# Moving a residual spill, half of a modulation part, two weight casts and one attention step inside the mixer of an encoder layer

## The chip, the core and the metric

The kernel runs on one core of one Trainium2 chip. The metric is the device time of one execution in microseconds (us); the median of three executions is 1164.8 us (1164.51 to 1168.15).

TensorE (PE in the profile, with its weight loads as PEld) multiplies, VectorE (DVE) and ScalarE (ACT) work on elements, GpSimd (POOL) helps with elements and issues some transfers, and SyncE (SP) issues most transfers. Each engine has a queue of its own that it works off strictly in order.

## The reference

One layer of an encoder for 512 prompt tokens and 32 sample tokens, all in float32, width 1024:

```python
mod = silu(c) @ w_cond + b_cond            # nine parts of 1024: shift, scale, gate of three blocks
x = LN(ALPHA*x + 0.5*(1+g1) * swiglu1(modulate(x, sh1, sc1)))
h = modulate(x, sh2, sc2)
rq,rk,rv,rg, aq,ak,av, iq,ik,iw = split(h @ w_in)
o_ret = head_norm(retention(rope(rq), rope(rk), rv)) * silu(rg)
s     = sum_h iw[h] * relu(iq[h] @ ik.T)   # indexer: scores of keys, 8 heads
o_att = attention over the top-k keys by s only
x = LN(ALPHA*x + (1+g2) * concat(o_ret, o_att) @ w_out)
x = LN(ALPHA*x + 0.5*(1+g3) * swiglu2(modulate(x, sh3, sc3)))
```

The gate g3 is part 8 of the modulation, the last of the nine. It is first needed after the second feed-forward block's products with gate and up weights.

## The kernel before

**Layout and precision.** Activations lie transposed, 128 channels on the partitions and the 544 tokens along the free side, in two halves of 272 tokens. Each float32 operand is split exactly into two parts, hi and lo, and a product is three matmuls (`mm3`, hi·hi, hi·lo, lo·hi). A weight tile of 128 columns and 1024 rows is therefore 24 matmuls for each half: 8 steps along the inner side, three matmuls each. All matmuls carry line 77 and all transposes line 80, because helpers issue them.

**Weights.** `fetch_w` loads a raw tile of 512 KB into one of three `wr` buffers from SP's queue. `split_w` makes the two parts in one of five `wh` buffers: ACT casts the raw tile to hi (L131), ACT writes minus hi into lo (L137), and POOL issues a transfer that adds the raw tile from memory into lo (L138). So lo is there only once this transfer has landed. `next_w` keeps three split tiles ahead of the one in use: the project that begins now also issues load, cast and transfer of the tile that is used three projects later.

**Order of the work.** The order on PE is written out by hand: `mm` and `turned` chain every PE instruction behind the one before. `load` chains the loads of SP's queue in the same way, in the order of the program. The other queues are ordered by the framework, which places an instruction by its place in the program and by its own reckoning of when the operands are there; `add_manual_dep(..., NOSYNC)` adds an order between two instructions and no wait. Side work runs as generators: `tick()` is called after each half of a project, and a generator that yields n is resumed n ticks later. What it then issues stands on PE's queue behind the half just done. In the mixer a tick is one half of a project, 24 matmuls.

**The mixer** (between the two feed-forward blocks) projects h with 33 tiles of `w_in`: first the indexer's key and queries, then for four retention heads query, key and value (`retention`), then for four attention pairs key, query and value (`pair_inputs`), then four gates. Alongside run:

- `cond_ahead(8)`, part 8 of the modulation. It loads eight row blocks `wc` of 512 KB and sums them, weighted, into two accumulators `ca` on DVE: two instructions of 128x1024 elements for each block (L587 and L589). The first four blocks are loaded from POOL's queue, the last four from SP's. `cond_done` then reduces the accumulators on DVE in four pieces (L546, L547) and with one matmul.
- `spill`: the residual `xr` (four tiles, 544 KB each) is written to memory and read back at the gates (`reload`).
- `queries` and `index_query`: the rotary part goes through small transfers (`rp`), DVE and back, then parts are made (L694 on ACT, L695 on DVE) and small copies run on POOL (L776).
- `indexer`: for each of ten steps (t, c) 12 or 6 matmuls for each pair of heads into two banks, one in tag `l` (two buffers) and one in tag `o` (one buffer). ACT takes each through relu (L814), and DVE sums them (L821, L823). The next step's second bank is free only after the relu of the second head of the pair (s = 1) has read it.
- `topk` on DVE (L853, L854), then `attention`: twelve steps (pair c, group n) of logits, softmax on DVE and ACT, transposes and values. A step of pair c may begin once `roped` has set the flag ("stack", c).

Tiles of all these kinds share one pool `up` of 35 buffers.

The tick count of the mixer, followed by hand through the code: `cond_ahead` is spawned at tick 130; the first four blocks are added at tick 132, the last four loaded at tick 140 and added at ticks 140, 144, 148 and 152; `cond_done` reduces at ticks 158 to 161. The spill is issued at tick 144, the indexer's step (1, 0) at tick 145 and (2, 0) at tick 146. `roped` of pair 0 runs at ticks 169 to 171, logits (0, 0) at tick 172.

Of the kernel before, what the change touches and what calls it, by code (L numbers as in the profile page):

```python
# [13 lines left out]
ALU = mybir.AluOpType  # L14
# [4 lines left out]
ND = D // P  # L19
# [20 lines left out]
def encoder_layer_kernel(ctx, tc, xT, cT, wc1, w_e, w_cond, b_condT, lnp, w_gu1, w_dn1, w_in, w_out, w_gu2, w_dn2,  # L40
                         ckT, cv, cikT, s0, cmat, ropes, dec, csm,
                         yT, akT, avT, ikT, st_p, st_s):
    nc = tc.nc
# [22 lines left out]
    last = {}  # L66
# [58 lines left out]
    def split_w(raw, n, name, lo_eng=None, pool=None, pin=False, src=None):  # L125
        if pool is None:
            hl = wh.tile([P, 2, ND, P], FR, name=f"wh_{name}", tag="wh")
            hi, lo = hl[:, 0], hl[:, 1]
        else:
            hi, lo = (pool.tile([P, ND, P], FR, name=f"wu_{name}", tag="u") for _ in range(2))  # L130
        c = nc.scalar.copy(hi[:, :n, :], raw[:, :n, :])  # L131
        if "relu" in last:
            tc.add_manual_dep(c.ins, last.pop("relu"), NOSYNC, reason="order of issue")
        if pin:
            tc.keep_in_program_order(c)
        if src is not None and lo_eng is None:
            nc.scalar.mul(lo[:, :n, :], hi[:, :n, :].bitcast(F32), -1.0)  # L137
            nc.gpsimd.dma_start(lo[:, :n, :], src, accum_op=ALU.add)  # L138
        else:
            r = (lo_eng or nc.gpsimd).tensor_tensor(lo[:, :n, :], raw[:, :n, :], hi[:, :n, :].bitcast(F32), op=ALU.subtract)  # L140
            last["lo"] = r.ins.name
        return hi, lo
# [7 lines left out]

    stream = []
    split = []
    fetched = []

    def fetch_ahead():
# [421 lines left out]
    def cond_ahead(m):  # L577
        acc = [up.tile([P, 1024], F32, name=f"ca{m}_{r}", tag="u") for r in range(2)]

        def part(d):  # L580
            return w_cond[d * P:(d + 1) * P, 1024 * m:1024 * m + 1024]

        def add(d, w):
            for r in range(2):
                c = cz[:, d, r:r + 1]
                if d == 0:
                    nc.vector.tensor_scalar(acc[r], w, c, None, op0=ALU.mult)  # L587
                else:
                    n = nc.vector.scalar_tensor_tensor(acc[r], w, c, acc[r], op0=ALU.mult, op1=ALU.add)  # L589
                    if d > 4:  # L590
                        tc.add_manual_dep(n.ins, last["pe"], NOSYNC, reason="pace")

        ws = [up.tile([P, 1024], F32, name=f"wc{m}_{d}", tag="u") for d in range(4)]
        for d in range(4):
            nc.gpsimd.dma_start(ws[d], part(d))
        yield 1
        for d in range(4):
            add(d, ws[d])
        yield 8
        for d in range(4, ND):  # L600
            ws.append(up.tile([P, 1024], F32, name=f"wc{m}_{d}", tag="u"))
            load(ws[d], part(d))
        for d in range(4, ND):
            add(d, ws[d])
            yield 4
        spawn(cond_done(m, acc))

    def known(*ms):
# [191 lines left out]
    def indexer():  # L800
        nc.vector.memset(work[0], 0.0)
        nc.vector.memset(work[0][0:64, 64:128], NEG)
        flags.add(("mask", 0))
        yield 0
        for t, c in ((1, 0), (2, 0), (1, 2), (2, 1), (2, 2), (2, 3), (3, 0), (3, 1), (3, 2), (3, 3)):
            L = P * (t + 1)
            acc = work[t]
            n = 512 // L
            pair = [bank("l", "isc"), bank("o", "isc")]
            pair_products([[p[:, L * e:L * e + L] for e in range(n)] for p in pair],  # L810
                          [(iq[c + e], iks, t) for e in range(n)])
            for s in range(2):
                rl = scr("rl")
                r = nc.scalar.activation(rl[:, :n * L], pair[s][:, :n * L], AF.Relu)  # L814
                if (t, c) == (1, 0):
                    last["relu"] = r.ins.name
                for e in range(n):
                    hh = 2 * (c + e) + s
                    r, f = rl[:, L * e:L * e + L], iw[:, t, hh:hh + 1]
                    if hh == 0:  # L820
                        nc.vector.tensor_scalar(acc, r, f, None, op0=ALU.mult)  # L821
                    else:
                        nc.vector.scalar_tensor_tensor(acc, r, f, acc, op0=ALU.mult, op1=ALU.add)  # L823
            yield 1
            if c + n == 4:
                nc.vector.memset(acc[0:64, L - 64:L], NEG)
                flags.add(("score", t))
                if t == 1:
                    spawn(topk())
        psA, psB = bank("a", "iss"), bank("o", "iss2")  # L830
        for g in range(2):
            ps, p2 = bank("l", "isg"), bank("t", "isg2")
            lq = iqz[:, 128 * g:128 * g + 128]
            mm(ps, lq, cik, start=True, stop=True)
            mm(p2[:, 0:32], lq, ikn, start=True, stop=True)
            rl = scr("rls")
            nc.vector.tensor_scalar(rl[:, 0:512], ps, 0.0, iws[:, g:g + 1], op0=ALU.max, op1=ALU.mult)
            nc.vector.tensor_scalar(rl[:, 512:544], p2[:, 0:32], 0.0, iws[:, g:g + 1], op0=ALU.max, op1=ALU.mult)
            yield 1
            mm(psA, sel, rl[:, 0:512], start=(g == 0), stop=(g == 1))  # L840
            mm(psB[:, 0:32], sel, rl[:, 512:544], start=(g == 0), stop=(g == 1))
        nc.scalar.copy(work['s'][:, 0:512], psA)
        nc.scalar.copy(work['s'][:, 512:544], psB[:, 0:32])
        flags.add(("score", 's'))
# [19 lines left out]
    project(taken(qs[3]))  # L864

    def spill():
        yield 3
        for j in range(4):
            load(xd[j], xr[j].rearrange("p a t -> p (a t)"))

# [156 lines left out]
    def pair_inputs(c):  # L1027
        qk = unit("aqk")
        k, q = qk[:, 0, :], qk[:, 1, :]
        st = [unit("aqs", FR), unit("aks", FR)]  # L1030
        V = unit("aV")
        kn = V[:, 1, 64:96]
        qz = V[:, 1, 0:64]
        nc.gpsimd.memset(qz, 0.0)

        rp = unit("rp")

        def roped():
            yield 0
            rope_turn(rp, k, q)  # L1040
            nc.sync.dma_start(akT[c], k)
            yield 1
            parts(st[1], k)
            nc.gpsimd.tensor_copy(kn, k[:, TP:T])
            parts(st[0], q)
            for s in range(2):
                nc.gpsimd.tensor_copy(qz[own(s), 32 * s:32 * s + 32], q[own(s), TP:T])
            yield 1
            flags.add(("stack", c))

        Vs[c] = V
        stacks[c] = st
        for slot, z in enumerate((k, q)):
            project(taken(z))
            rope_gather(rp, slot, z)
        spawn(roped())
        value_chunk(V[:, 0, 0:512], V[0:32, 1, 128:256], avT[c], ("pair", c))

# [553 lines left out]
```

## Time and profile before

| what | value |
|---|---|
| time, median of three executions | 1164.8 us |
| the profiled execution's own time | 1163.95 us |
| its span, first to last instruction | 1162.1 us |
| PE busy | 1131.8 us (97%) |
| DVE busy | 785.7 us (68%) |
| ACT busy | 620.5 us (53%) |
| POOL busy | 202.9 us (17%) |
| mean granted clock of PE | 0.99 |

Busy shares are taken over the span. A row of the timeline gives start, length, engine, line, operation and tiles (written tile, arrow, read tiles) of one group, how many instructions it merges, and in brackets how long the engine stood before it and what released it. A row of the waits gives the waiting engine, tile and line, the releaser, the sum, the number and the longest. A row of the windows gives the stretch, its length, and for each engine busy time and count, then the granted clock of PE (1.00 is full), the share of time in which the transfer engines were busy, and GB/s. Rows marked SPq are issues of transfers on SP's queue, not their landing.

### The profile page before, as it was taken

The page shows a single profiled execution, that of the slowest core. Times are in us where ns is not written, and L with a number is a line of the kernel's source. Part 1 is how long each engine was busy: PE and PEld are TensorE (multiplying, and loading weights), DVE is VectorE, ACT ScalarE, POOL GpSimd, SP SyncE. Part 2 cuts the span into 40 slices and gives each one's busy share as a digit, 9 for nine tenths or more (in the row PEclk, how much of TensorE's full clock was granted, in tenths as well). Part 3 has the DMA queues.
Part 4 walks back from the last instruction along what each step waited for, and adds up shares of the span by engine and source line. Part 5 has one row for each costly group of instructions (what it writes and reads, how often), then busy time and mean ns, then how long its engine had stood idle before and what let it go on. Part 6 is the DMA issues. An engine that isn't in the chain of part 4 may idle for free.

```text
span 1162.1 us, 22904 instructions
## 1 busy us (share of the span) xinstructions
PE 1131.8 (97%) x9203; PEld 1099.8 (95%) x9203; DVE 785.7 (68%) x1738; ACT 620.5 (53%) x1064; POOL 202.9 (17%) x229
## 2 busy tenths in 40 slices
PE   8999999999999999799999999999999999999995
PEld 7999999999999999688989988999999999999995
DVE  5667674772569387588988777689877777821416
ACT  3545444443435435465655758654776667753523
POOL 0122111111211301432311101110211111061110
PEclk9999999999999999899999999999999999999998
DMA  9899999986999746874664757871777777478842
GB/s 357 291 290 317 255 263 230 243 218 165 299 276 240 160 175 155 273 175 119 147 149 84 193 177 210 227 193 66 157 180 166 180 183 175 116 224 192 178 83 78
DMA packets 71739, 228.26 MB, mean 196 GB/s; under 512 B 8688, under 2 KB 12912, under 8 KB 71632
## 3 DMA queue, kind: packets, MB, share of 16 engines
q0 software_dynamic: 23184, 77.87, 37.8%
q1 hardware_dynamic: 48304, 148.79, 36.2%
q8 instruction: 72, 1.18, 0.4%
q14 instruction: 35, 0.29, 0.1%
q10 hardware_dynamic: 144, 0.14, 0.0%
HBM read 215.16 MB, written 9.58 MB: 193 GB/s over the span
## 4 chain that ended last, share of the span: by engine, by line
PE 88%; DMA 5%; DVE 4%; ACT 1%; POOL 1%; issue 1%; SPq 0%; DVEq 0%; POOLq 0%; ACTq 0%
PE dn L77 26%; PE gu L77 23%; PE in L77 14%; PE pA L77 9%; PE pB L77 5%; DMA we_raw<-in_w_e 3%; PE pC L77 2%; PE gu_e L77 2%; PE po L77 1%; PE pt L80 1%; PE lg L77 1%; DMA wh_w<-in_w_in 1%; DMA rp<-iqf 1%; PE ro L77 1%; PE isc L77 1%
## 5 line engine op out<-in xcount | busy, mean ns | idle before, releaser
L77 PE MATMUL dn<-hid,wh_w 128*128 128x272 f32 x2112 | 266.8, 288 | 0.0
L77 PE MATMUL gu<-h,wh_w 128*128 128x272 f32 x2112 | 265.8, 288 | 0.0
L77 PEld LDWEIGHTS dn<-hid,wh_w 128*128 128x128 f32 x2112 | 265.4, 188 | 0.2
L77 PEld LDWEIGHTS gu<-h,wh_w 128*128 128x128 f32 x2112 | 264.9, 188 | 0.0
L77 PE MATMUL in<-h,wh_w 128*128 128x272 f32 x1392 | 190.7, 294 | 4.4 <-DMA wh_w<-in_w_in 3.9
L77 PEld LDWEIGHTS in<-h,wh_w 128*128 128x128 f32 x1392 | 179.9, 191 | 10.3 <-DMA wh_w<-in_w_in 4.2
L131 ACT CAST wh_w<-wr_w 128x1024 fp32r<-128x1024 f32 (+1 forms) x126 | 128.0, 1019 | 113.3 <-PE dn L77 87.7
L572 DVE SCALAR_TENSOR_TENSOR ca<-wc,cz,ca 128x1024 f32<-128x1024 f32 x84 | 106.4, 1294 | 25.7 <-DMA wc<-in_w_cond 25.6
L137 ACT ACTIVATE wh_w<-wh_w 128x1024 fp32r<-128x1024 f32 (+1 forms) x116 | 119.6, 1033 | 2.2
L138 POOL DMA_DIRECT2D wh_w<-in_w_gu x43 | 37.8, 878 | 201.6 <-ACT wh_w L137 162.0
L138 POOL DMA_DIRECT2D wh_w<-in_w_dn x42 | 37.0, 893 | 183.9 <-ACT wh_w L137 175.6
L281 DVE SCALAR_TENSOR_TENSOR xs<-dn,C,xs 128x272 f32<-128x272 f32 (+2 forms) x24 | 9.0, 404 | 81.2 <-PE dn L77 81.2
L77 PE MATMUL pA<-hs,wh_s 128*128 128x272 f32 x432 | 60.0, 288 | 0.0
L201 DVE TENSOR_TENSOR tnh<-tnh,gu 128x272 f32<-128x272 f32 x44 | 19.2, 436 | 56.3 <-PE gu L77 56.3
L77 PEld LDWEIGHTS pA<-hs,wh_s 128*128 128x128 f32 x432 | 56.3, 188 | 0.0
L202 ACT CAST hid<-tnh 128x272 fp32r<-128x272 f32 x52 | 21.5, 419 | 61.4 <-DVE tnh L201 61.4
L138 POOL DMA_DIRECT2D wh_w<-in_w_in x29 | 25.3, 874 | 148.2 <-ACT wh_w L137 90.3
L199 ACT ACTIVATE tnh<-gu 128x272 f32<-128x272 f32 x44 | 17.5, 398 | 54.9 <-PE gu L77 54.4
L1284 POOL DMA_DIRECT2D wh_g<-in_w_gu x18 | 15.7, 874 | 157.7 <-ACT wh_g L1283 97.6
L1318 ACT COPY s<-pA 128x272 f32<-128x272 f32 x54 | 20.8, 386 | 36.9 <-PE pA L77 35.5
L853 DVE MAX8 m<-wk 128x8 f32<-128x544 f32 (+3 forms) x65 | 38.6, 596 | 0.7
L854 DVE MATCH_REPLACE8 wk<-m,wk 128x544 f32<-128x544 f32 (+3 forms) x65 | 38.0, 584 | 0.0
(330 smaller groups left out, 1847.9 us busy)
## 6 DMA issues: line engine op xcount, KB each, us to landing
wc<-in_w_cond SPq DMA_DIRECT2D x52, 512.0 KB, 6.6
wr_w<-in_w_gu SPq DMA_DIRECT2D x48, 512.0 KB, 6.3
wh_w<-in_w_gu POOLq DMA_DIRECT2D x43, 512.0 KB, 7.8
wr_w<-in_w_in SPq DMA_DIRECT2D x33, 512.0 KB, 5.8
wh_w<-in_w_in POOLq DMA_DIRECT2D x29, 512.0 KB, 6.9
wr_w<-in_w_dn SPq DMA_DIRECT2D x32, 448.0 KB, 4.1
wh_w<-in_w_dn POOLq DMA_DIRECT2D x28, 448.0 KB, 6.5
wr_g<-in_w_gu SPq DMA_DIRECT2D x18, 512.0 KB, 3.6
```

The lines of the kernel that those rows point to most:

```text
L77: ordered("pe", nc.tensor.matmul(*a, **kw))
L131: c = nc.scalar.copy(hi[:, :n, :], raw[:, :n, :])
L137: nc.scalar.mul(lo[:, :n, :], hi[:, :n, :].bitcast(F32), -1.0)
L138: nc.gpsimd.dma_start(lo[:, :n, :], src, accum_op=ALU.add)
L199: nc.scalar.activation(t, pg, AF.Tanh, scale=0.5)
L201: nc.vector.tensor_tensor(t, t, pu, op=ALU.mult)
L202: nc.scalar.copy(hid[:, 0, a:b], t)
L572: nc.vector.scalar_tensor_tensor(acc[r], w, c, acc[r], op0=ALU.mult, op1=ALU.add)
L853: behind(behind(nc.vector.max(m8, w), "pe"), "norm")
L854: nc.vector.match_replace(w, in_to_replace=m8, in_values=w, imm_value=MARK)
L1284: nc.gpsimd.dma_start(lo, src, accum_op=ALU.add)
L1318: pin(nc.scalar.copy(s, ps))
```

## The change

Four edits, all in the order of issue; no operation on data is added or taken out.

1. `spill` waits 32 ticks in place of 3: the four writes are issued at tick 173.
2. `cond_ahead`: the first four blocks are added at ticks 137 to 140, one a tick; the last four are loaded at tick 155 and added at ticks 155, 160, 165 and 170; `cond_done` reduces at ticks 197 to 200 and issues its matmul at tick 204. Every add is ordered behind the last PE instruction issued (before, only those of blocks 5 to 7).
3. Every cast of a weight is noted in `casts`. At the indexer's step (1, 0) the two youngest are ordered behind the relu of s = 1; they are the casts of the key and the value weights of retention head 1. (The next cast issued after it, that of query 2, was ordered behind this relu before, and still is.)
4. `roped` of pair 0 sets its flag a tick later, so that logits (0, 0), (0, 1) and (0, 2) come at ticks 173 to 175.

```diff
@@ split_w
         c = nc.scalar.copy(hi[:, :n, :], raw[:, :n, :])
+        casts.append(c.ins)
         if "relu" in last:
             tc.add_manual_dep(c.ins, last.pop("relu"), NOSYNC, reason="order of issue")
...
     split = []
+    casts = []
     fetched = []
@@ cond_ahead
                 c = cz[:, d, r:r + 1]
                 if d == 0:
-                    nc.vector.tensor_scalar(acc[r], w, c, None, op0=ALU.mult)
+                    n = nc.vector.tensor_scalar(acc[r], w, c, None, op0=ALU.mult)
                 else:
                     n = nc.vector.scalar_tensor_tensor(acc[r], w, c, acc[r], op0=ALU.mult, op1=ALU.add)
-                    if d > 4:
-                        tc.add_manual_dep(n.ins, last["pe"], NOSYNC, reason="pace")
+                tc.add_manual_dep(n.ins, last["pe"], NOSYNC, reason="pace")
...
-        yield 1
+        yield 6
         for d in range(4):
             add(d, ws[d])
-        yield 8
+            yield 1
+        yield 14
         for d in range(4, ND):
             ws.append(up.tile([P, 1024], F32, name=f"wc{m}_{d}", tag="u"))
             load(ws[d], part(d))
         for d in range(4, ND):
             add(d, ws[d])
-            yield 4
+            yield 5 if d < ND - 1 else 25
         spawn(cond_done(m, acc))
@@ indexer
                 r = nc.scalar.activation(rl[:, :n * L], pair[s][:, :n * L], AF.Relu)
-                if (t, c) == (1, 0):
+                if (t, c, s) == (1, 0, 1):
+                    for cast in casts[-2:]:
+                        tc.add_manual_dep(cast, r.ins.name, NOSYNC, reason="order of issue")
                     last["relu"] = r.ins.name
@@ spill
-        yield 3
+        yield 32
         for j in range(4):
             load(xd[j], xr[j].rearrange("p a t -> p (a t)"))
@@ pair_inputs, roped
-            yield 1
+            yield 2 if c == 0 else 1
             flags.add(("stack", c))
```

## The prediction

> **What bounds the kernel now.** I read the page first, for which engine is full, then who makes that engine wait, then the timeline of each queue around the longest waits.
>
> ```profile
> span 1162.1 us, 22904 instructions
> PE 1131.8 (97%) x9203; PEld 1099.8 (95%) x9203; DVE 785.7 (68%) x1738; ACT 620.5 (53%) x1064; POOL 202.9 (17%) x229
> ```
>
> TensorE is busy 1131.8 of 1162.1 us. No edit takes a matmul away, so only the 30.3 us in which it stands, and stretches in which its matmuls run slowly, can be won. The waits of PE, longest first, begin so (waiting tile, releaser, sum, times, longest):
>
> ```profile
> PE in L77 <- DMA wh_w<-in_w_in: 3.9, 1, 3.9
> PE isc L77 <- ACT rl L814: 3.0, 1, 3.0
> PE lg L77 <- ACT aqs L694: 2.0, 1, 2.0
> PE rkt L80 <- ACT rv L884: 1.5, 1, 1.5
> ```
>
> All four lie in the mixer, and each happens once. PE's timeline shows two groups:
>
> ```profile
> 477.56 1.32 PE L77 MATMUL isc<-iks,iqs 64*128 64x384 f32 x5 [3.01 <-ACT rl L814]
> 478.82 0.82 PE L77 MATMUL in<-h,wh_w 128*128 128x272 f32 x2
> 483.54 4.51 PE L77 MATMUL in<-h,wh_w 128*128 128x272 f32 x22 [3.90 <-DMA wh_w<-in_w_in]
> ...
> 490.94 3.26 PE L77 MATMUL in<-h,wh_w 128*128 128x272 f32 x24
> ...
> 607.59 0.44 PE L77 MATMUL lg<-aks,aqs 64*128 64x128 f32 x4 [2.03 <-ACT aqs L694]
> 608.50 0.73 PE L77 MATMUL lg<-aks,aqs 64*128 64x128 f32 x8 [0.47 <-DVE aqs L695]
> 609.16 4.80 PE L77 MATMUL in<-h,wh_w 128*128 128x272 f32 x24
> ```
>
> Group 1: the indexer's step (2, 0) waits 3.01 us for a bank that a relu must empty. Then two matmuls of query 1 (the query tile of retention head 1) run with hi, and the third, which needs lo, waits 3.90 us for the landing of POOL's transfer. Group 2: logits (0, 0) wait 2.03 and 0.47 us for the parts of pair 0. After each group the same matmuls are slower: 22 in 4.51 us and 24 in 4.80 us, where 24 take 3.26 us otherwise. This loss of clock is part of the price: 4.51 - 22/24 x 3.26 = 1.52 us and 4.80 - 3.26 = 1.54 us. Group 1 costs 3.01 + 3.90 + 1.52 = 8.43 us, group 2 2.03 + 0.47 + 1.54 = 4.04 us.
>
> Why is group 1 late? ACT, SP and POOL at that time:
>
> ```profile
> 473.16 1.05 ACT L131 CAST wh_w<-wr_w 128x1024 fp32r<-128x1024 f32 x1 [4.68 <-DMA wr_w<-in_w_in]
> ...
> 475.96 1.04 ACT L131 CAST wh_w<-wr_w 128x1024 fp32r<-128x1024 f32 x1
> 476.90 0.61 ACT L814 ACTIVATE rl<-isc 128x512 f32<-128x512 f32 x1
> ```
>
> ```profile
> 456.34 1.06 SPq L74 DMA_DIRECT2D wc<-in_w_cond  x2
> ...
> 464.11 2.21 SPq L74 DMA_DIRECT2D wc<-in_w_cond  x2
> 466.37 0.42 SPq L74 DMA_DIRECT2D wr_w<-in_w_in  x1
> ...
> 469.71 3.81 SPq L74 DMA_DIRECT2D x_spill<-xr  x4
> ```
>
> ```profile
> 467.28 3.34 POOL L776 COPY misc<-iqf 64x32 f32<-64x32 f32 x4
> ...
> 475.71 0.89 POOL L138 DMA_DIRECT2D wh_w<-in_w_in  x1 [0.91 <-ACT vz L877]
> ...
> 482.50 0.47 POOL L776 COPY misc<-iqf 64x32 f32<-64x32 f32 x2 [2.78 <-DMA iqf<-rp]
> ```
>
> ACT stands 4.68 us at the cast of query 1, whose raw tile lands only at 473.16; the relus that free PE are queued behind it, the second behind key 1's cast too (475.96). The raw tile is late because its load (466.37) stands on SP's queue behind the four `wc` loads. The lo transfer is late because it follows that cast and because POOL issues it at 475.71, behind small copies. The landing times of this stretch, from the transfers' view of 425 to 625 us (KB each, median us from issue to landing):
>
> ```profile
> wh_w<-in_w_in POOLq DMA_DIRECT2D x23, 512.0 KB, 7.1
> wr_w<-in_w_in SPq DMA_DIRECT2D x21, 512.0 KB, 6.7
> x_spill<-xr SPq DMA_DIRECT2D x4, 544.0 KB, 7.2
> wc<-in_w_cond SPq DMA_DIRECT2D x4, 512.0 KB, 4.7
> ```
>
> **The change, part by part.** *The wc loads and the spill leave SP's queue here; the casts of key 1 and value 1 go behind the relus.* The load of query 1 moves up to the place of the first or the second pair of `wc` loads, 456.34 or 464.11; with 6.7 us of landing the tile is there at 463.0 or 470.8, not 473.16. So the cast no longer holds the relus, and key 1's cast is ordered behind them: the 3.01 us go. Next late is lo. Without the relu wait PE begins at 477.56 - 3.01 = 474.55; five small matmuls at full clock (about 0.7 us, half of 1.32) and two of query 1 (0.27) bring it to lo at 475.5. Lo lands 7.1 us behind its issue, and this depends on POOL's order: issued ahead of the four copies (467.3) it lands at 474.4 and PE waits 0; behind them (470.6) at 477.7, a wait of 2.2; in its old place (475.71) at 482.8, a wait of 7.3, no less than both old waits together. The copies should shorten, though: four took 3.34 us while two took 0.47 later, and DVE's adds ran then, the slowest of which also took nearly twice the median (min/median/max in ns):
>
> ```profile
> L589 DVE SCALAR_TENSOR_TENSOR ca<-wc,cz,ca x14: 1272/1279/2325, 441.9 to 517.9; 128x1024 f32<-128x1024 f32 x14
> ```
>
> I take a wait of 1.0 us, between the two early places, since the cast that POOL follows becomes 2 to 10 us earlier. A gap of 1.0 should leave the clock whole. Group 1 gives 8.43 - 1.0 = 7.4 us; bounds 0 and 8.4. Key 1's cast now follows relus that should end near 472; with cast and second pass (2 x 1.04 us) and 7.1 of landing its lo is there near 482, and PE comes to key 1 two halves (6.5 us) and their side work after 475.5: 0, at most 1 if POOL is late, and that lies within the bounds above. The 1.5 us of `rkt`, where ACT is late behind casts, may go too: bounds 0 and 1.5, I take 0.7.
>
> The Trainium skill, page "DMA: Bandwidth & Descriptors", section "Queues, rings and completion order", says that each transfer engine takes turns between the queues that have work, packet by packet; by this the spill on SP's queue can slow POOL's transfer only by its turn. The trace fits it: the late lo landed 7.8 us behind its issue (475.71 to 483.54), the median is 7.1. So I credit the spill's leaving with nothing for that transfer.
>
> *Logits a step later.* Between the transposes and logits (0, 0) PE now runs a half of the next project, 3.26 us, whose weight is split three projects ahead. Logits begin at 607.59 - 2.03 + 3.26 = 608.8; the parts were complete at 608.50. The cover is 0.3 us, thin: the add of block 7, 2 x 1.279 = 2.6 us of DVE at tick 170, may stand ahead of these parts and would bring back up to 2.3 us. I take 0.2 left and 3.8 us won of 4.04; bounds 1.7 and 4.0. The later steps have spare ticks before pair 1 begins at tick 178, so nothing is passed on.
>
> The Trainium skill, page "TensorE: Matmul & The Clock Gate", Part 1, puts the fall to half clock behind an idle window of about 3.4 us. The gap here was 2.03 us and the matmuls after it were still slow, so the measured row decides: the 1.54 us belong to the group. By the rule alone they would not, and the gain would be 1.5 us less.
>
> *The adds on DVE.* Blocks 0 to 3 move into ticks 137 to 140, where DVE waited for the rotary transfer; no price. Blocks 4 to 7 go to ticks 155 to 170, about 531 to 602 us:
>
> ```profile
> 531.00:606.00 75.00, 74.56 (x577) 69.72 (x575) 63.88 (x213) 41.44 (x77) 17.07 (x18) 1.00 0.65 154
> 726.00:744.00 18.00, 18.00 (x173) 17.67 (x172) 9.73 (x23) 14.46 (x21) 3.58 (x5) 1.00 1.01 260
> ```
>
> ```profile
> 548.34 0.70 DVE L546 STREAM_TRANSPOSE ctr<-ca 128x512 f32<-128x512 f32 x1
> 549.07 0.69 DVE L547 TENSOR_REDUCE red<-ctr 128x16 f32<-128x512 f32 x1
> ```
>
> DVE (third busy figure) has 75.00 - 63.88 = 11.1 us idle there. In come 8 x 1.279 = 10.2 us, out go four pieces of `cond_done`, 4 x 1.39 = 5.6: it fits by 6.5 us. PE hides behind its three banks; each add may cost it between 0 and the 0.47 us for which it waited on a DVE part above, 1.9 in all; I take 0.6. Block 4 is added in the tick in which it is loaded: DVE may stand for the 4.7 us of landing, and all evacuations queued behind it with it; bounds 0 and 4.7, I take 0.5, since the three banks cover 3 x 3.26 us. `cond_done` at 726 to 744 meets 18.00 - 9.73 = 8.3 us of idle DVE for its 5.6: 0, up to 5.6 if it slips into the layer norm behind; I take 0.3. The loads of wc at 535 and the spill near 614 meet transfer engines with room (0.65 busy in the row above); 0. The pool: I count 34 to 35 of 35 buffers in use from tick 144 to 150 (four more for `xr`, fewer for `wc`) and two more than before through ticks 186 to 195 (`ca`); bounds 0 and 3.0 (the relu wait, a wait for a buffer too), I take 0.2.
>
> **Sum.** 7.4 + 0.7 + 3.8 = 11.9 won, 0.6 + 0.5 + 0.3 + 0.2 = 1.6 lost: 10.3 us. From the profiled execution's 1163.95 (1.85 around its span) that is 1153.65; the median of the runs is 0.85 above that execution, and I forecast 1164.8 - 10.3 = 1154.5.
>
> **Rivals.** *A. POOL's order stays.* Lo is issued last of POOL's work as before and its wait takes the place of both old ones; group 1 gives 0 to 1, and 0.5 + 0.7 + 3.8 - 1.6 = 3.4 is left: 1161.4, between 1160 and 1162.5. For it: the row at 475.71 stands behind copies that have nothing to do with the cast. Against it: POOL's place follows the expected time of the cast, and that moves up. Chance 0.18.
>
> *B. Nothing moves.* The waits only change their names (lo for relu, and DVE's parts for ACT's): 1163 to 1166. Chance 0.07.
>
> *C. Slower: DVE stands at its adds.* SP's queue itself waits long for DVE in this stretch:
>
> ```profile
> SPq L955 <- DVE Dm L953: 38.6, 3, 23.0
> ```
>
> If the `wc` loads of tick 155 stand behind such a store of up to 23.0 us and an add is queued on DVE meanwhile, DVE stands; past the 9.8 us that three banks cover each further us is PE's. To end 3.5 us above 1164.8 it must lose 13.8 us, so stand 23.6 us: 1168 to 1170, just past the longest wait shown. Chance 0.08.
>
> *D. The clock rule.* The slow half behind the logits has another cause than the gap and stays: 1154.5 + 1.5 = 1156.0. Against it: none of the rows shown has a slow half without a gap ahead of it. Chance 0.06.
>
> **The numbers.** The forecast has 0.61. A measurement of this kernel can tell about 0.3% (3.5 us) from no change. Faster by more: forecast, D and rather over half of A, 0.77; within: the rest of A and B, 0.15; slower: C, 0.08. The range runs from all gains and no costs, 8.4 + 1.5 + 4.0 = 13.9 won (1150.9), to the top of A: 1150.8 to 1162.5; outside lie B, C and a little of the forecast.
>
> **What would show it.** Right: no PE wait of over 1.2 us between 470 and 500 us and none at logits (0, 0); 24 matmuls behind each in some 3.3 us; POOL's transfer for query 1 ahead of the last copies; `x_spill` issued some 140 us later than 469.71. Wrong: a PE wait on `wh_w` of over 3 us near 476 (A), DVE waiting on `wc` between 525 and 560 (C), a PE wait on `nm` or `xq` near 700 to 790 that grew (the pool, `cond_done`).

## The result, and the profile after

The changed kernel takes 1156.58 us (median of five executions, 1153.90 to 1159.47) against 1164.8 us for the kernel before on the same chip (five executions, 1162.80 to 1168.15). The ratio is 0.9926, 95% interval 0.9902 to 0.9951: 8.2 us faster. The profiled execution of the changed kernel is its slowest, 1159.47 us.

The head of its page, and the first rows of the waits of PE (waiting tile, releaser, sum, times, longest):

```profile
span 1157.6 us, 22910 instructions
PE 1131.0 (98%) x9203; PEld 1100.0 (95%) x9203; DVE 787.6 (68%) x1738; ACT 619.8 (54%) x1064; POOL 202.2 (17%) x229
```

```profile
PE dn L77 <- DMA wh_w<-in_w_dn: 2.5, 1, 2.5
PE lg L77 <- DVE mx L1026: 2.3, 2, 1.2
PE lg L77 <- ACT aqs L696: 1.6, 1, 1.6
PE in L77 <- DMA wh_w<-in_w_in: 1.4, 1, 1.4
```

PE is as busy as before and stands less. The two longest waits of before, 3.9 us on the lo part of query 1 and 3.0 us on a relu, are gone. The `dn` row lies ahead of the mixer, where both kernels issue the same work in the same order; two of the runs below have it too (2.8 us each: the third edit alone, and the run with the logits a tick later), the other eleven profiles not. Here it makes the mixer begin 4.4 us later (below), and it says nothing of the change. The logits' rows are still there. Of the 2.3 us on `mx`, a masked row maximum of the softmax, 1.07 us lie near 697 us, where the kernel before waited 1.14 us on `nm`; the other 1.19 us, at the first logits, are new.

PE's timeline at the places of group 1 and group 2:

```profile
451.76 0.41 PE L77 MATMUL in<-h,wh_w 128*128 128x272 f32 x2
453.61 3.01 PE L77 MATMUL in<-h,wh_w 128*128 128x272 f32 x22 [1.43 <-DMA wh_w<-in_w_in]
...
475.24 0.98 PE L77 MATMUL isc<-iks,iqs 64*128 64x256 f32 x12
476.15 3.25 PE L77 MATMUL in<-h,wh_w 128*128 128x272 f32 x24
479.33 0.79 PE L77 MATMUL isc<-iks,iqs 64*128 64x384 f32 x6
480.06 3.29 PE L77 MATMUL in<-h,wh_w 128*128 128x272 f32 x24
483.19 1.05 PE L77 MATMUL rs<-rqk 128*128 128x128 f32 x8
...
485.51 3.27 PE L77 MATMUL in<-h,wh_w 128*128 128x272 f32 x24
...
489.93 0.28 PE L80 MATMUL rkt<-cm,rqk 128*32 128x128 f32 x1 [0.42 <-DVE rv L891]
...
600.46 0.44 PE L77 MATMUL lg<-aks,aqs 64*128 64x128 f32 x4 [1.57 <-ACT aqs L696]
601.19 0.73 PE L77 MATMUL lg<-aks,aqs 64*128 64x128 f32 x8 [0.29 <-DVE aqs L697]
601.85 4.80 PE L77 MATMUL in<-h,wh_w 128*128 128x272 f32 x24
...
608.21 0.79 PE L77 MATMUL lg<-aks,aqs 64*128 64x384 f32 x5 [1.19 <-DVE mx L1026]
608.93 4.79 PE L77 MATMUL in<-h,wh_w 128*128 128x272 f32 x24
```

Group 1 has no wait left: the two halves of query 1 (480.06 and 485.51) run in 3.29 and 3.27 us. A new wait of 1.43 us stands at the second weight tile of the mixer. Group 2 is worse: logits (0, 0) still wait, 24 matmuls still take 4.80 us, and one step on there is another wait of 1.19 us with another slow half.

SP, ACT and POOL show why group 1 is clean:

```profile
425.16 21.90 SPq L74 DMA_DIRECT2D wr_w<-in_w_in  x5
...
472.36 1.38 SPq L74 DMA_DIRECT2D wr_w<-in_w_in  x3
```

```profile
453.81 1.05 ACT L131 CAST wh_w<-wr_w 128x1024 fp32r<-128x1024 f32 x1 [3.31 <-DMA wr_w<-in_w_in]
...
476.25 1.09 ACT L816 ACTIVATE rl<-isc 128x512 f32<-128x512 f32 x2 [0.51 <-PE isc L77]
477.22 2.00 ACT L131 CAST wh_w<-wr_w 128x1024 fp32r<-128x1024 f32 x2
```

```profile
457.39 1.80 POOL L139 DMA_DIRECT2D wh_w<-in_w_in  x2 [6.54 <-PE piws L80]
469.47 0.85 POOL L778 COPY misc<-iqf 64x32 f32<-64x32 f32 x2 [10.28 <-DMA iqf<-rp]
```

Query 1's raw tile is the fifth of the loads that begin at 425.16 (before, four stood together there and query 1's came at 466.37); the row merges them, and this fifth one is issued at 446.73. Its cast is at 453.81, its lo is the second of the two that POOL issues from 457.39 (at 458.3), 11 us ahead of the first copy, and the casts of key 1 and value 1 (477.22) follow the relus (476.25).

The stages of the mixer, from the starts of four rows of PE's timeline in each profile (first `in` with a `wh_w` tile, first `isc`, first `rs`, first `lg`) and the span; the last four columns are their differences. "1", "2" and "3" are the edits by the numbers of the list above.

| kernel | `in` | `isc` | `rs` | `lg` | span | in to isc | isc to rs | rs to lg | lg to end |
|---|---|---|---|---|---|---|---|---|---|
| before | 447.33 | 469.97 | 487.89 | 607.59 | 1162.1 | 22.64 | 17.92 | 119.70 | 554.51 |
| changed | 451.76 | 475.24 | 483.19 | 600.46 | 1157.6 | 23.48 | 7.95 | 117.27 | 557.14 |
| 2 alone | 447.10 | 470.46 | 479.26 | 604.99 | 1161.6 | 23.36 | 8.80 | 125.73 | 556.61 |
| 1 alone | 447.70 | 471.77 | 488.72 | 606.15 | 1161.2 | 24.07 | 16.95 | 117.43 | 555.05 |
| 1 and 3 | 446.91 | 469.75 | 485.32 | 603.09 | 1158.3 | 22.84 | 15.57 | 117.77 | 555.21 |
| 1 and 2 | 447.12 | 470.33 | 480.44 | 598.51 | 1156.3 | 23.21 | 10.11 | 118.07 | 557.79 |
| 2, spill 5 ticks later | 447.67 | 471.01 | 480.44 | 598.49 | 1154.7 | 23.34 | 9.43 | 118.05 | 556.21 |
| changed, adds 4 ticks apart | 447.12 | 470.43 | 478.38 | 596.32 | 1151.2 | 23.31 | 7.95 | 117.94 | 554.88 |
| 1 and 3, `wc` one tick later | 447.38 | 470.07 | 486.20 | 604.04 | 1159.3 | 22.69 | 16.13 | 117.84 | 555.26 |
| adds 4 apart, `wc` loads early | 447.01 | 470.58 | 478.52 | 602.20 | 1158.8 | 23.57 | 7.94 | 123.68 | 556.60 |

From before to changed: +0.84, -9.97, -2.43 and +2.63, together -8.93 us. The spans differ by 4.5 only because the mixer began 4.43 us later in this execution; the medians differ by 8.2.

### The profile page after: what moved, and what is told of

The parts are those of the page before. It is cut to its first block, busy times and chain, and to the rows that moved or that the text cites. A ratio compares the mean times of both kernels' runs of the same rounds, so it can differ in the third digit from the quotient of the medians.

```text
span 1157.6 us, 22910 instructions
## 1 busy us (share of the span) xinstructions
PE 1131.0 (98%) x9203; PEld 1100.0 (95%) x9203; DVE 787.6 (68%) x1738; ACT 619.8 (54%) x1064; POOL 202.2 (17%) x229
## 4 chain that ended last, share of the span: by engine, by line
PE 83%; DMA 7%; DVE 5%; ACT 3%; issue 1%; SPq 0%; POOL 0%; DVEq 0%; ACTq 0%; POOLq 0%
PE dn L77 25%; PE gu L77 22%; PE in L77 12%; PE pA L77 9%; PE pB L77 5%; DMA we_raw<-in_w_e 3%; PE pC L77 2%; PE gu_e L77 2%; DMA wr_w<-in_w_in 2%; PE po L77 1%; PE pt L80 1%; DMA wh_w<-in_w_gu 1%; ACT wh_w L131 1%; PE lg L77 1%; PE ro L77 1%
## 5 line engine op out<-in xcount | busy, mean ns | idle before, releaser
L857 DVE MAX8 m<-wk 128x8 f32<-128x544 f32 (+3 forms) x65 | 38.6, 595 | 0.6
L858 DVE MATCH_REPLACE8 wk<-m,wk 128x544 f32<-128x544 f32 (+3 forms) x65 | 38.0, 584 | 0.0
```

Of the source, the lines that this page charges most:

```text
L857: behind(behind(nc.vector.max(m8, w), "pe"), "norm")
L858: nc.vector.match_replace(w, in_to_replace=m8, in_values=w, imm_value=MARK)
```

## The experiments

All ratios are against the kernel before, on the same chip and in the same job.

### The edits one by one: 2 alone

Theory 1 was that the four `wc` loads on SP's queue ahead of query 1's load are the whole cause. The edit is the second of the diff above, nothing else.

> The kernel before with the second edit alone (weight blocks 4 to 7 of the modulation part loaded and added later); spill, cast order and logits as before. Theory 1 (the four wc loads on SP's queue ahead of query 1's load are the whole cause): query 1's raw tile is loaded behind the other weight loads, its cast no longer stands between PE and the relus, lo is issued ahead of POOL's copies; the PE waits of 3.01 and 3.90 us are gone and 24 matmuls behind them take 3.3 us; 1164.8 - 8.4 = 1156.4, so 1155 to 1158. Rival 1 (the traffic of the spill makes the transfers of query 1 late): the 3.90 us on lo stay in part, 1159 to 1162. Rival 2 (the place of the cast of key 1 ahead of the second relu is the cause): the 3.01 us stay and with them the slow half, 1160 to 1162.

Measured: 1164.35 us, ratio 0.9999 (0.9988 to 1.0010). The mechanism came and the gain did not. From isc to rs it took 8.80 us as foreseen, and from rs to the logits 6.0 us more than before:

```profile
489.04 0.28 PE L80 MATMUL vts<-cm,vz 128*32 128x128 f32 x1 [2.87 <-ACT rsA L939]
...
492.39 0.40 PE L80 MATMUL rkt<-cm,rqk 128*32 128x128 f32 x1 [2.89 <-DVE rv L887]
```

```profile
467.36 0.44 SPq L74 DMA_DIRECT2D wr_w<-in_w_in  x1
467.84 3.32 SPq L74 DMA_DIRECT2D x_spill<-xr  x4
474.82 0.53 SPq L676 DMA_DIRECT2D iqf<-rp  x1
475.39 1.06 SPq L74 DMA_DIRECT2D wr_w<-in_w_in  x2
```

```profile
482.94 1.05 ACT L131 CAST wh_w<-wr_w 128x1024 fp32r<-128x1024 f32 x1 [1.44 <-DMA wr_w<-in_w_in]
...
488.30 0.68 ACT L939 ACTIVATE rsA<-rkt,misc 128x512 f32<-128x512 f32 x1
```

Value 1's raw load, the first of the two at 475.39, stands behind the spill and behind a gather that waits for DVE: the spill's issues take 3.32 us, and SP then stands until 474.82 for the gather. ACT waits for that tile at the cast (482.94), and `rsA`, which PE needs, is queued behind the casts. PE came 8.6 us sooner and met the next load that was late. Theory 1 falls as the whole cause.

### 1 alone, 3 alone, and all but 2

```diff
     def spill():
-        yield 3
+        yield 32
```

> The kernel before with the first edit alone (residual spilled 29 ticks later). Theory 1: query 1's load still stands behind the four wc loads, both waits of group 1 stay, 3.01 and 3.90 us; 1164 to 1166. Rival 1 (the spill's traffic): lo lands sooner, the wait of 3.90 us shrinks by 2 us or more, 1160 to 1163.

Measured: 1160.70 us, 0.9964 (0.9952 to 0.9976): the rival's time, but lo's wait shrank by 0.6 us and not by 2. Its profiled execution is the slowest of five (1162.94), so the stages show only a part: -0.97 from isc to rs and -2.27 from rs to the logits. Query 1's lo:

```profile
477.73 1.03 POOL L138 DMA_DIRECT2D wh_w<-in_w_in  x1 [1.44 <-ACT vz L877]
```

```profile
484.10 4.78 PE L77 MATMUL in<-h,wh_w 128*128 128x272 f32 x22 [3.29 <-DMA wh_w<-in_w_in]
```

It landed 6.4 us behind its issue, 7.8 before (7.0 and 8.4 in the two runs with the third edit below, without and with the spill in this stretch). The larger part lies behind rs, where value 1's load no longer stands behind the spill: the wait of 1.51 us at `rkt` is 0.75.

Next the third edit alone:

```diff
-                if (t, c) == (1, 0):
+                if (t, c, s) == (1, 0, 1):
+                    for cast in casts[-2:]:
+                        tc.add_manual_dep(cast, r.ins.name, NOSYNC, reason="order of issue")
                     last["relu"] = r.ins.name
```

> The kernel before with the third edit alone (casts of key 1 and value 1 behind the relus of indexer step (1, 0)). Theory 1: the first relu still stands behind query 1's cast, which waits for its raw tile until 473.2; only the 1.04 us of key 1's cast go from the wait of 3.01, and lo's wait grows by as much, since PE comes to it sooner; 1163.8 to 1165. Rival 2 (cast order is the cause): the wait of 3.01 us is gone, and the slow half with it, 1159 to 1161.

Measured: 1164.86 us, 1.0003 (0.9989 to 1.0018), as theory 1 had it but for the size. The relu's wait shrinks from 3.01 to 0.32 us, and lo's grows from 3.90 to 6.44 us. The execution that was profiled is the longest of twelve (1172.87) and is not used for stages.

Then both of these, with the loads and adds of `wc` as before:

> The changed kernel without the second edit: spill, cast order and logits as changed, the four wc loads where they were. Theory 1: nothing of the 8.2 us is left but what the cast order gives by itself, 1162.5 to 1165.5, and the two waits stand near 476 and 480 us with 6 to 7 us in all. Rivals 1 and 2 together (spill and cast order carry it): 1156 to 1159.

Measured: 1161.69 us, 0.9966 (0.9955 to 0.9978): the gain of edit 1 alone and no more, which theory 1 had not allowed for. The two waits are 0.27 and 5.08 us, 5.4 in all, where 6 to 7 were expected.

### 1 and 2 together, the casts left where they were

The fourth edit alters nothing: built without it, the changed kernel has the same instructions in the same order on all five queues. So the changed kernel without the third edit is edits 1 and 2.

> The changed kernel without the third edit (casts of key 1 and value 1 where they were); since the fourth edit alters no instruction, these are the first and the second edit together, whose runs alone gave 0.9964 and 0.9999. Theory 2 (the loads that ACT's casts wait for stand on SP's queue behind both the wc loads and the spill, so each edit alone only moves the wait: the wc loads' going wins 9.1 us from isc to rs, and the spill, left in place, gives 6.0 back by value 1's load behind it): both waits of group 1 are gone and the waits of 2.87 us at vts and 2.89 us at rkt are gone too; 1155.5 to 1158.5. Rival (the cast order is what the second edit needs): the waits at vts and rkt stay with 2 us or more each, 1161 to 1165.

Measured: 1159.34 us, 0.9952 (0.9938 to 0.9967), theory 2 in kind and 0.8 us above its range. The waits at `vts` and `rkt` are gone and rs to logits is 118.07 us. One wait of 1.77 us is left at the indexer:

```profile
476.63 0.79 PE L77 MATMUL isc<-iks,iqs 64*128 64x384 f32 x5 [1.77 <-ACT rl L814]
```

On ACT's queue the casts of key 1 and value 1 (471.29 and 473.34) stand ahead of the relus (475.51); the third edit moves both behind them: 10.11 to 7.95 us, 2.2 us. So edits 2 and 3 are each worth nothing alone, edit 1 is worth 4 us, and the three together 8.2 (edits 2 and 3 without 1 were not run).

### Place on the queue, or traffic? The spill only 5 ticks later

```diff
 (edit 2 alone)
-        yield 3
+        yield 8
         for j in range(4):
             load(xd[j], xr[j].rearrange("p a t -> p (a t)"))
```

> The kernel before with the second edit, and the spill issued 5 ticks later (tick delay 8, not 32): its four transfers then stand on SP's queue behind the loads of key 1, value 1 and the next tile, but still run in this stretch. Theory 2 (the place on SP's queue): the waits of 2.87 and 2.89 us at vts and rkt, which the second edit alone had, are gone as with the spill 29 ticks later; from rs to the logits 118 us, not 125.7; as the first and second edit together (0.9952), 0.994 to 0.9965. Rival (the traffic of the spill beside the loads, or the buffers it frees late): the two waits stay with 2 us or more each, from rs to the logits over 122 us, 0.998 to 1.001.

Measured: 1157.51 us, 0.9936 (0.9923 to 0.9949), just under the theory's range; rs to logits 118.05 us, no wait of 2 us there. The spill's 2.1 MB still move in this stretch, but behind the raw loads of key 1, value 1 and query 2. It is enough that the spill is issued behind them. This puts value 1's load ahead of the gather as well, so the run shows that the place on the queue counts, not how its price divides between the spill and the gather.

### `wc` one tick later

```diff
 (edits 1 and 3)
         for d in range(4):
             add(d, ws[d])
-        yield 8
+        yield 9
```

> The changed kernel without the second edit, but with the four wc loads (and the adds of blocks 4 to 7, still 4 ticks apart) one tick later than in the kernel before: query 1's load then stands ahead of them on SP's queue, and all their transfers and adds still run in the indexer's stretch. Theory 1 (place on the queue, for the loads): from isc to rs 8 to 9 us, not 15.6, no wait over 1.5 us on wh_w or rl between 470 and 485 us; the adds no longer meet the logits, so no wait of 1.2 us on mx there; 0.990 to 0.994. Rival (the 2 MB of wc or the eight adds on DVE beside POOL's copies are what made group 1 late): the wait on wh_w of 4 to 5 us stays, 0.996 to 0.998.

Measured: 1160.52 us, 0.9964 (0.9953 to 0.9975). The time lies in the rival's range, but neither had the mechanism. Query 1's load went ahead and the waits on `wh_w` and on the relu are gone; a third wait took their place, and a wait of 1.23 us on `mx` came that theory 1 had excluded:

```profile
475.97 1.82 PE L77 MATMUL isc<-iks,iqs 64*128 64x256 f32 x10 [5.51 <-DVE iks L697]
```

```profile
471.70 2.48 DVE L591 SCALAR_TENSOR_TENSOR ca<-wc,cz,ca 128x1024 f32<-128x1024 f32 x2 [7.14 <-DMA wc<-in_w_cond]
474.10 1.82 DVE L697 TENSOR_TENSOR iks<-ix,iks 128x512 fp32r<-128x512 f32 x1
```

```profile
467.74 2.02 SPq L74 DMA_DIRECT2D wc<-in_w_cond  x4
```

The `wc` loads now stand on SP's queue behind gathers (467.74). DVE reaches the add of block 4 first and stands 7.14 us at it, and the parts that the indexer needs are queued behind the add. This is rival C of the prediction, at another place.

### `wc` early, the adds far away

```diff
 (the changed kernel, adds 4 ticks apart as below)
             add(d, ws[d])
             yield 1
-        yield 14
         for d in range(4, ND):
             ws.append(up.tile([P, 1024], F32, name=f"wc{m}_{d}", tag="u"))
             load(ws[d], part(d))
+        yield 14
```

> The run with the adds at ticks 155, 159, 163 and 167, but with the four wc loads issued at tick 141, one tick later than in the kernel before: on SP's queue they stand behind query 1's load and ahead of those of key 1 and value 1, and their 2 MB move in the indexer's stretch; only the adds are far away. Theory 1, as mended by the run with one tick (it is enough that query 1's load goes ahead, if DVE has no add that waits for a block): from isc to rs 8 to 9 us, no wait of over 1.5 us there, and DVE waits for no wc; 0.989 to 0.992, as with the loads 15 ticks later (0.9897). Rival (the 2 MB of wc beside the transfers of query 1, key 1 and value 1 are what made the group late): waits on wh_w or rl of 2 us or more in this stretch, 0.993 to 0.996.

Measured: 1159.91 us, 0.9960 (0.9946 to 0.9974): the rival's time, and the theory as mended is wrong too. Isc to rs is 7.94 us, so query 1 is served. But the raw tiles of key 1 and value 1 stand behind 2 MB of `wc`. The transfers' view (KB each, median us to landing) of the three loads here, and then of the same three in the changed kernel:

```profile
wr_w<-in_w_in SPq DMA_DIRECT2D x3, 512.0 KB, 7.3
```

```profile
wr_w<-in_w_in SPq DMA_DIRECT2D x3, 512.0 KB, 4.6
```

```profile
475.95 1.05 ACT L131 CAST wh_w<-wr_w 128x1024 fp32r<-128x1024 f32 x1 [3.28 <-DMA wr_w<-in_w_in]
```

ACT stands 3.28 us at key 1's cast, and PE pays at the indexer (1.14 us for a relu) and at `rkt` (2.44 us and a slow half): rs to logits 123.68 us. What the runs bear out is wider than theory 1. Three casts were late because their raw load was issued behind `wc` or the spill: query 1's behind `wc` (473.16 before, 449.23 with edit 2 alone), value 1's behind the spill and a gather (482.94 with edit 2 alone, 473.34 with edits 1 and 2), key 1's behind `wc` (475.95 here, 472.40 with the loads at tick 155). All of ACT's queue behind the cast is then late.

### The logits: a tick later in truth

```diff
-            yield 2 if c == 0 else 1
+            yield 3 if c == 0 else 1
             flags.add(("stack", c))
```

> The changed kernel with the flag for the logits of pair 0 one tick later still, which puts a half of the next project (24 matmuls, 3.26 us) between the transposes and logits (0, 0). Theory: the waits of 1.57 and 0.29 us and the 1.54 us of slow matmuls behind them go, 3.4 us; the wait of 1.19 us on mx may go too with its slow half, 1.5 + 1.2 more, since DVE's search then is a half further on; 1150.5 to 1153.2. Rival: the parts of pair 0 are no longer late, but the products behind the last step also slip by a half and hold a bank or a buffer longer, so that the waits reappear at the next logits; 1155 to 1157.5.

Measured: 1155.62 us, 0.9927 (0.9913 to 0.9940), no change from the changed kernel: the rival.

```profile
602.82 0.96 PE L77 MATMUL lg<-aks,aqs 64*128 64x128 f32 x12
603.71 3.25 PE L77 MATMUL in<-h,wh_w 128*128 128x272 f32 x24
610.25 0.69 PE L77 MATMUL lg<-aks,aqs 64*128 64x384 f32 x1 [3.29 <-DVE mx L1026]
612.10 1.32 PE L77 MATMUL lg<-aks,aqs 64*128 64x384 f32 x5 [1.17 <-DVE mx L1026]
```

Logits (0, 0) wait for nothing and are followed by a half of 3.25 us, as the prediction had it. The next step then waits 4.5 us for DVE, which must empty the banks: its first masked copy (L1026) begins at 606.40, 2.6 us behind the last of the matmuls, because instructions of the search stand ahead of it on DVE's queue.

### The adds of block 7 away from the logits

```diff
-            yield 5 if d < ND - 1 else 25
+            yield 4 if d < ND - 1 else 28
```

> The changed kernel with blocks 5, 6 and 7 of the modulation part added at ticks 159, 163 and 167, not 160, 165 and 170; the end of the part stays at its tick. Theory 3 (the two adds of block 7 push the search and the masked copies of the logits back on DVE, and PE waits for the bank): the wait of 1.19 us on mx near 608 us goes, with the 1.53 us of slow matmuls behind it, and those of 1.57 and 0.29 us stay; 1156.6 - 2.7 = 1153.9, so 1153 to 1155. Rival: the same 2.5 us of DVE's time stand ahead of the rotary step of pair 0 instead, the parts come later by as much, and the wait moves there; 1156 to 1158.5.

Measured: 1152.99 us, 0.9897 (0.9884 to 0.9910), the fastest of all. The interval overlaps that of the changed kernel (0.9902 to 0.9951) at its edge. In the changed kernel DVE has

```profile
594.54 1.27 DVE L591 SCALAR_TENSOR_TENSOR ca<-wc,cz,ca 128x1024 f32<-128x1024 f32 x1
```

and a second such add at 596.34, ahead of the parts and the search; with the adds at tick 167 they are gone from there, and so is the wait on `mx`:

```profile
596.32 0.44 PE L77 MATMUL lg<-aks,aqs 64*128 64x128 f32 x4 [0.84 <-ACT aqs L696]
597.24 0.73 PE L77 MATMUL lg<-aks,aqs 64*128 64x128 f32 x8 [0.48 <-DVE aqs L697]
597.90 4.81 PE L77 MATMUL in<-h,wh_w 128*128 128x272 f32 x24
602.63 1.16 PE L77 MATMUL lg<-aks,aqs 64*128 64x384 f32 x6
```

Logits to end is 554.88 us against 557.14: 2.3 us of the 2.7 expected. How adds that are over before the logits begin can hold a bank, DVE's rows show; these are the two masked copies that empty the banks of the second logits, in the changed kernel and then here:

```profile
605.88 0.41 DVE L1026 CUSTOM_DVE_ANT_0 Pu<-lg,wk 128x256 f32<-128x256 f32 x1
...
607.73 0.41 DVE L1026 CUSTOM_DVE_ANT_0 Pu<-lg,wk 128x256 f32<-128x256 f32 x1
```

```profile
601.94 0.40 DVE L1026 CUSTOM_DVE_ANT_0 Pu<-lg,wk 128x256 f32<-128x256 f32 x1
...
602.53 0.40 DVE L1026 CUSTOM_DVE_ANT_0 Pu<-lg,wk 128x256 f32<-128x256 f32 x1
```

With the adds at tick 170 a pass of the search (L858 and L857) stands between the two copies; here they are 0.59 us apart. The adds thus cost by the order that the framework then gives DVE's queue.

Then 3 ticks apart:

```diff
-            yield 5 if d < ND - 1 else 25
+            yield 3 if d < ND - 1 else 31
```

> The changed kernel with blocks 5 to 7 of the modulation part added 3 ticks apart (158, 161, 164), the end of the part at its old tick. Theory 3 (only the two adds of tick 170, beside the search and the masked copies, cost): as with 159, 163 and 167, no wait on mx near the first logits; 0.9885 to 0.991. Rival (the 3.6 us of the run with 4 ticks were chance, or any place of the adds costs as much elsewhere): 0.992 to 0.994.

Measured: 1154.41 us, 0.9906 (0.9890 to 0.9921); logits to end 554.66 us, no wait on `mx` there. The second such run says the same. All four profiles with unmoved logits and the adds of block 7 at tick 170 have the wait on `mx`, 1.2 to 2.7 us. Without them six have none, and two have 1.2 us all the same: the two runs above that load `wc` at tick 141. The masked copies tell why. The second one begins 7.26 or 7.27 us behind the start of logits (0, 0) in the four profiles with the adds at tick 170, and 6.01 to 6.21 us behind it in the other eight. So the adds make the bank 1.1 to 1.3 us later in every case. In the six without a wait the half behind logits (0, 0) is slow (4.37 to 4.81 us), and PE comes to the bank when it is free; in the two others this half takes 3.26 us, and PE comes sooner and waits.

Then the adds 4 ticks apart and the flag of pair 0 at `yield 3`, both in one kernel:

> The last two together: logits of pair 0 a tick later, and the adds at ticks 155, 159, 163 and 167. Theory: 3.4 + 2.7 = 6.1 us, PE waits for nothing over 0.5 us between rs and the last logits of pair 0; 1150 to 1152. Rival (the two win the same 2.7 us): no better than the better of the two, 1152.5 to 1154.5.

Measured: 1157.00 us, 0.9930 (0.9914 to 0.9946). Worse than its rival: the wait on `mx` is 3.37 us although no add stands near. With the logits a half later, passes of the search alone stand ahead of the masked copies on DVE's queue: the first begins 3.66 us behind the start of the logits, not 2.24 as in the run with the adds alone. The two edits do not add.

## Why the prediction was right, and where it was not

The forecast was 1154.5 us with 10.3 us won; measured were 1156.58 and 8.2. The total is near partly by luck: a step that failed (the logits, with the adds) was made up by one that was too small (group 1).

**Group 1: right, and too small.** Forecast 7.4 us, measured 9.97 from isc to rs. The 3.01 and 3.90 us went, with the slow half behind them (1.52 us). Beside these the five small and two large matmuls between the two waits had been slow too: 1.32 us for five against 0.79, and 0.82 for two against 0.27, another 1.1 us that the sum had missed. The remaining wait of 1.0 us did not come, because query 1's load moved further ahead than thought, to the other raw loads that begin at 425.16. It is issued at 446.73, which is 442.3 counted from a mixer that begins as before; the prediction had 456.34 or 464.11. A wait that was not foreseen came: PE stands 1.43 us at 453.61 for the second weight tile's lo, and the stage to isc is 0.84 us longer. The same wait, 1.1 to 1.8 us, is in all nine profiles in which the first four blocks are added at ticks 137 to 140, and in none of the five in which they are added at tick 132. The run with `wc` one tick later has query 1's load moved and the adds at tick 132, and not the wait; so the load's move alone does not bring it. In the nine, POOL issues the next two lo transfers 2.8 us behind the one that PE waits for, in the other five 4.5 us. Whether that is the cause was not tried.

**The cause of group 1: half right.** The prediction gave the gain to the `wc` loads' leaving and to the order of the casts. Edit 2 alone gave 0.9999: the spill takes the gain back by standing, with a gather, ahead of value 1's load. "So I credit the spill's leaving with nothing for that transfer" is the step that failed, and the sum has no other term for the spill; edit 1 alone gives 0.9964, and the run with the spill 5 ticks later shows that its place is what counts, not that it is gone. The Trainium skill, page "DMA: Bandwidth & Descriptors", section "Queues, rings and completion order", has the transfer engines take turns between queues; the prediction used it for POOL's lo alone and did not ask what stands behind the spill on its own queue. For lo itself the landing went from 7.8 to 6.4 us without the spill (8.4 to 7.0 with the third edit), so the spill beside it on the other queue was not free either.

**`rkt`: right.** Forecast 0.7, measured 1.51 to 0.42 us; the 0.46 us of the indexer's wait on DVE went as well. With the 0.46 us less at the first logits this is 2.0 of the 2.4 us from rs to logits.

**The logits: wrong.** Forecast 3.8 us won; the two waits shrank by 0.6 us in all, the slow half stayed, and 2.6 us were lost from logits to end. The step that failed is "Between the transposes and logits (0, 0) PE now runs a half of the next project". Followed through the construction of the program, the flag is set at tick 171 before and at 172 after, but attention sees it at tick 172 in both: before, `roped` is resumed behind attention in the tick, and after the longer yield it is resumed ahead of it. So the fourth edit issues nothing differently, and the prediction, and the list of edits above with it, had read ticks 173 to 175 off the code. Had the tick been real, 3.8 us would have been wrong too: its run won the two waits and lost as much one step later. The term was also mis-sized by the 1.54 us of slow matmuls. Where the half behind logits (0, 0) ran in 3.26 us and the adds were away, PE waited 1.23 and 1.24 us for DVE's masked copy instead, and the project behind the second logits began 7.56 to 7.60 us behind the first; with the slow half it began 7.2 to 7.4 us behind. DVE, not the clock, set the pace there.

**The adds on DVE: right in kind, mis-sized and misplaced.** Forecast 0.6 us for eight adds; measured are 2.3 us for the two of tick 170 (557.14 against 554.88), with which the second masked copy comes over 1 us later, and no wait over 0.6 us near the others in the run that moves them. The price was bounded by 0.47 us an add because that was the longest wait on a DVE part; the bank that a masked copy holds was not looked at. The 0.5 us for add 4 did not come: the loads stand at 507.91 on SP's queue, not at tick 155, and the add is at 526.74. That this cover was real, and C's mechanism too, the run with one tick shows: 7.14 us of DVE, 5.51 us of PE.

**Pool and `cond_done`:** no wait of theirs is in the profile; 0.5 us too much. The spill is issued at 568.66, 99 us later and not 140: the framework placed it ahead of its tick.

**Rivals.** A did not come, since POOL issues lo 11 us ahead of the copies. Its ground, that the copies held lo back, was a misreading: POOL had stood 0.91 us idle at 475.71, and ACT's second pass on query 1's tile ended only at 475.31. B is what edit 2 and edit 3 do, each by itself. D's 1156.0 is close to the measurement, but its mechanism was not seen: the slow half stayed and so did its gap, and in both runs where the gap is gone the half takes 3.25 us.

## What to carry to other kernels

On a queue that works in order, what counts is which loads stand behind a transfer, not which engine waits now: after moving one transfer away, follow the next load that the consumer's cast needs, because the engine that comes sooner meets it sooner. An edit that delays a flag is worth reading out of the built order, since two schedules with different ticks may be the same program. A wait or a slow stretch is worth its length only if no other engine's wait ends right behind it. Extra work on a second engine should be kept away from the few places where a bank is waiting to be emptied, even if that engine has idle time on average.

## What the runs showed of the hardware

The loss of clock behind the logits is not in proportion to the gap. The granted clock of PE in one window of 2 us behind logits (0, 0), in the changed kernel and then in the run with the adds 4 ticks apart (stretch, length, busy times with counts, clock, share of the transfers, GB/s):

```profile
604.00:606.00 2.00, 2.00 (x12) 2.00 (x12) 2.00 (x9) 0.53 (x3) 0.78 (x1) 0.56 0.24 23
```

```profile
600.00:602.00 2.00, 2.00 (x10) 2.00 (x10) 2.00 (x9) 0.52 (x3) 0.62 (x1) 0.50 0.42 47
```

The clock is 0.56 and 0.50. Gaps of 1.57 and 0.29 us cost 4.80 - 3.26 = 1.54 us of slow matmuls; gaps of 0.84 and 0.48 us cost 4.81 - 3.26 = 1.55, so shortening the gap won its own length and nothing more. In four runs (edits 1 and 2, edit 2 with the spill 5 ticks later, and the two that load `wc` at tick 141) gaps of 1.63 to 1.75 and 0.29 us at the same place were followed by a half in 3.26 us; in the first of them the granted clock from 600 to 602 us is 1.00. At the second weight tile single gaps of 1.14 to 1.52 us were followed by 22 matmuls in 3.01 to 3.04 us in eight profiles, and one of 1.76 us by 22 in 4.55 us. The Trainium skill, page "TensorE: Matmul & The Clock Gate", Part 1, has the clock set by a free-running window of about 3.4 us; a loss of about 1.5 us for a stretch at half clock, and a gap that counts in one run and not in another, would fit such a window. That a window with only 1.3 us of standing brings half clock is not what "idle" there suggests; the matmuls between these gaps are small (64x128), and whether they count as activity no run here settles.

In the two views of three loads above, a raw tile of 512 KB lands in 4.6 us with nothing large ahead of it on SP's queue and in 7.3 us behind 2 MB of `wc`. The two runs that differ only in where these loads stand are at 0.9960 and 0.9897, 6.9 us apart in their medians: 2.7 us of landing and the place on the queue become a wait of 3.28 us on ACT, then 2.44 us and a slow half on PE, then the late logits.
